# Two buffers for a convolution's copies, stores from another queue, and low parts of weights made half by VectorE and half by GpSimd

## The chip, the cores and the metric

The kernel runs on one core of one Trainium2 chip. The metric is device time in microseconds of one execution, the median of several runs. Engines are named as the profile names them: PE (TensorE), DVE (VectorE), ACT (ScalarE), POOL (GpSimd) and SP (SyncE, which here issues most transfers).

## The reference

The program computes two blocks on 512 tokens of 1024 channels: attention with a feed-forward layer, then a block of two branches (a gated depthwise convolution and a bidirectional state-space scan), followed by a mixture of 16 experts. The change lies in the second block's two branches:

```python
proj = einsum('btd,dk->btk', rms_norm(h, w_norm_mix), w_in)      # conf_a, conf_g, z, xbc, dt, gates
c = conf_a * sigmoid(conf_g)
c = depthwise_conv(c, w_conf_dw, b_conf_dw)                       # 31 taps, 1024 channels
branch_conf = silu(layer_norm(c)) @ w_conf_out
xbc = silu(depthwise_conv(xbc, w_ssm_conv, b_ssm_conv))           # 7 taps, 3072 channels
y = bidir_ssd(xs, dt, ..., Bs, Cs, ssm_d)                         # chunks of 128 tokens, 4 groups
branch_ssm = rms_norm(y * silu(z), w_ssm_norm) @ w_ssm_out
h = h + (gates[:D] * branch_conf + gates[D:] * branch_ssm) @ w_out
```

All inputs are float32.

## The kernel before, in words

Tokens lie along the free axis, in two halves of 264 (`HS`, 528 tokens with the meta tokens). Every projection is done by `lin2h`: a 128x1024 chunk of weights is loaded by SP into `wraw` (three buffers), ACT rounds it into a high part `whi` (L109, two buffers), and POOL subtracts that from `wraw` to get the low part `wlo` (L110, two buffers). PE then runs 48 matmuls per chunk, three for each of eight row blocks and each half: high by low (L142), low by high (L143), high by high (L144). ACT can write `whi` only after PE has done with the chunk two before.

After the norm, the stage makes the state-space inputs and runs four groups `g` of the scan. In each group a list of 16 steps (`ssd_steps`: `pre` on ACT, DVE and POOL, `mm` on PE) is laid out by hand, and `fill` spreads the other work evenly between the steps: the next group's convolved inputs (`convs`, whose seven taps per tile are DVE multiply-adds, L749, handed out by `background`), tiles of the gated product (`conf_tile`), the depthwise convolution's tiles (`conf_conv`), `z_tile` and `gate_tile`. PE's instructions run in this written order. The order on the other engines is made by the scheduler of the tile framework, which takes data dependences and buffers into account.

`conf_tile(m)` writes its product to DRAM (`rcD`). `conf_conv(m)` copies it back into `cz` in four pieces shifted by one token each (L909), loads its weights `cw` (L913), and runs 64 matmuls for each half of the tokens (L922) in which four taps lie on the partitions; the result `co` is stored to `cfD` (L928). `fetch(0)` stands ahead of the first half, `fetch(1)` is called when the first half's matmuls have been issued. Both `cz` and `cw` have one buffer. `gate_tile` stores its gate to `gD` (L951). In a scan step `y_rows` loads two broadcast rows (L817), `y_pre` makes the decay factors from them (ACT L830, DVE L833, POOL L842), and `y_mm` multiplies (L853); between the states of two chunks POOL and DVE carry `pv` on (L810, L811), and POOL makes `xe` (L798) for the states' matmuls (`stp`, L806). The rows of step j are loaded at the `pre` of two steps before. `ssp` is the stage's pool of buffers; `rp` are the inputs of the taps, cleared at their ends by POOL (L737).

Of the kernel before, what the change touches and what calls it, by code (L numbers as in the profile page):

```python
# [9 lines left out]
F32 = mybir.dt.float32  # L10
# [3 lines left out]
AF = mybir.ActivationFunctionType  # L14
# [3 lines left out]
P = 128  # L18
D = 1024
S = 512  # L20
T = 528
TH = 264
# [8 lines left out]
HS = [(0, TH), (TH, T)]  # L31
# [15 lines left out]
HALVES = (382, 383)  # L47
OFF = None
NBS = 6
NB = 6  # L50
LAMBDA_INIT = 0.8 - 0.6 * math.exp(0.0)
PV = {}
# [16 lines left out]
def body(ctx, tc, a, out):  # L69
    nc = tc.nc  # L70
    pe, act, dve, pool, sp = nc.tensor, nc.scalar, nc.vector, nc.gpsimd, nc.sync
# [20 lines left out]
    upool = pools(ctx)("upool", side="right")  # L92
    hpool = pools(hs)("hpool", side="right")

    wlast = []

    def wload(src, e):
        raw = wp.tile([P, 1024], F32, name="wraw", tag="wraw", bufs=3)
# [3 lines left out]
    def wchunk(src, kc, n=WC, raw=None):  # L102

        raw = raw or wload(src, kc * n)
        hi = wp.tile([P, 1024], F32R, name="whi", tag="whi", bufs=2)
        lo = wp.tile([P, 1024], F32R, name="wlo", tag="wlo", bufs=2)
        e = kc * n
        with tc.high_priority(OFF):
            act.copy(hi[:, :e], raw[:, :e])  # L109
            pool.tensor_sub(lo[:, :e], raw[:, :e], hi[:, :e])  # L110
        r = lambda t: t[:, :e].rearrange("p (k n) -> p k n", k=kc)
        return r(hi), r(lo)

# [14 lines left out]
    def V(name, i=0, n=1):  # L128
        o, w = PV[name]
        return pv[:, o + i:o + i + n]  # L130
# [343 lines left out]
    for u in range(len(units) + 2):  # L474
        if u < len(units):
            h, qi = units[u]
# [8 lines left out]
        if u >= 2:  # L485
            h, qi = units[u - 2]
# [49 lines left out]
    for m in range(NFF):  # L536
        pss = []
        for wn in ("w_gate", "w_up"):
            w = wchunk(a[wn][m], KD)
            ps = lin2.tile([P, 512], F32, name="fps", tag="f")  # L540
# [41 lines left out]
    w = wchunk(wd(KD - 1, 0), 8)  # L582
    for h in range(2):
        down_part(0, w, h)
    w = [wchunk(wd(KD - 1, i), (8, 6)[i - 1]) for i in (1, 2)]
# [53 lines left out]
    ssp = pools(b2s)("ssp")  # L639
# [74 lines left out]
    for h in range(2):  # L714
        for k in range(KD):
            for pss, wv, n in ((first[0], dtv, 64), (first[1], wB, P)):
                ps, s0, s1 = pss[h]
# [12 lines left out]
    def conv_ssm(tiles, first=None):  # L730

        rps = []

        def unit(i):
            m, dst = tiles[i]
            rp = ssp.tile([P, T + 6], F32, name="rp", tag="rp", bufs=3)
            pool.memset(rp[:, :3], 0.0)  # L737
            pool.memset(rp[:, T + 3:], 0.0)
            for ps, s0, s1 in (first if i == 0 and first else lin2h(lambda i: W2[32 + m], U)):
                act.activation(rp[:, 3 + s0:3 + s1], ps[:, :TH], AF.Copy, scale=0.5)  # L740
            act.activation(dst, rp[:, :T], AF.Identity, bias=hv[:, m:m + 1], scale=V("sw", m * 7))
            rps.append(rp)
            if i:
                for k in range(1, 7):
                    for x in range(2):
                        soon.append(lambda k=k, x=x: tap(k, *tiles[x], rps[x]))

        def tap(k, m, dst, rp):
            dve.scalar_tensor_tensor(dst, rp[:, k:k + T], V("sw", m * 7 + k), dst, ALU.mult, ALU.add)  # L749
            if k == 6:  # L750
                th = ssp.tile([P, T], F32, name="th", tag="th", bufs=2)
                act.activation(th, dst, AF.Tanh)
                dve.scalar_tensor_tensor(dst, th, 1.0, dst, ALU.add, ALU.mult)

        return [lambda: unit(0), lambda: unit(1)]
# [8 lines left out]
    def ssd_steps(g):  # L764
# [48 lines left out]
        def y_rows(c, q):  # L813
            n = CH[c][1] - CH[c][0]
            for d in range(2):
                row = ssp.tile([P, 4, P], F32, name=f"row{d}", tag=f"row{d}", bufs=3)
                sp.dma_start(out=row[:, :, :n], in_=rowD[d, c, 8 * g + 4 * q:8 * g + 4 * q + 4, :n].partition_broadcast(P))  # L817
                keep["row", c, q, d] = row
# [43 lines left out]
        pre, mm = [], []  # L862
# [7 lines left out]
        for j, (c, q) in enumerate(Y):  # L870
            pre.append([lambda c=c, q=q: y_pre(c, q)])
            mm.append([lambda c=c, q=q: y_mm(c, q)])
            pre[j + 4].insert(0, lambda c=c, q=q: y_rows(c, q))
            if q == 0 and c != CO[-1]:
                mm[-1].append(lambda c=c: cross(CO[CO.index(c) + 1]))
        return pre, mm

    cfD = dram.tile([P, KD, T], F32, name="cfD")
    rcD = dram.tile([KD, P, T + 31], F32, name="rcD")

    def conf_tile(m):

        th = []

        def gate_half():
            th.append(ssp.tile([P, T], F32, name="ct", tag="ct", bufs=1))
            for ps, s0, s1 in lin2h(lambda i: W2[8 + m], U):
                act.activation(th[0][:, s0:s1], ps[:, :TH], AF.Tanh, scale=0.5)

        def value_half():  # L890
            rp = ssp.tile([P, T + 31], F32, name="rcp", tag="rcp")
            pool.memset(rp[:, :15], 0.0)
            pool.memset(rp[:, T + 15:], 0.0)
            for ps, s0, s1 in lin2h(lambda i: W2[m], U):
                dve.scalar_tensor_tensor(rp[:, 15 + s0:15 + s1], th[0][:, s0:s1], 1.0, ps[:, :TH], ALU.add, ALU.mult)
            sp.dma_start(out=rcD[m], in_=rp)

        return [gate_half, value_half]

    def conf_conv(m):  # L900


        o = []

        def fetch(h):
            s0, s1 = HS[h]
            z = ssp.tile([P, 4, TH + 28], F32, name="cz", tag="cz")
            for j in range(4):
                sp.dma_start(out=z[32 * j:32 * j + 32],  # L909
                             in_=rcD[m][:, s0 + j:s1 + j + 28].rearrange("(b c) t -> c b t", c=32))  # L910
            if h == 0:
                w = ssp.tile([P, 8, 4, 32], F32, name="cw", tag="cw")
                sp.dma_start(out=w, in_=a["conf_dw"][m].rearrange("p (i b c) -> p i b c", i=8, b=4))  # L913
                o.extend((ssp.tile([P, T], F32, name="co", tag="co"), w, None))
            o[2] = z

        def taps(h):
            s0, s1 = HS[h]
            ps = lin.tile([P, 512], F32, name="l3", tag="lin")
            for i in range(8):  # L920
                for b in range(4):
                    pe.matmul(ps[32 * b:32 * b + 32, :TH], o[1][:, i, b, :], o[2][:, b, 4 * i:4 * i + TH],  # L922
                              start=i == 0, stop=i == 7, skip_group_check=True)
            act.activation(o[0][:, s0:s1], ps[:, :TH], AF.Identity, bias=V("cb", m), scale=0.5)
            if h == 0:
                fetch(1)
            else:
                sp.dma_start(out=cfD[:, m, :], in_=o[0])  # L928

        return [lambda: fetch(0), lambda: taps(0), lambda: taps(1)]  # L930

    def z_tile(m):
        th = ssp.tile([P, T], F32, name="zt", tag="zt")
# [10 lines left out]
    gD = dram.tile([16, P, T], F32, name="gD")  # L944

    def gate_tile(m, pl):
        th = pl.tile([P, T], F32, name="gt", tag="gt", bufs=1 if pl is ssp else 2)
        for ps, s0, s1 in lin2h(lambda i: W2[56 + m], U):
            act.activation(th[:, s0:s1], ps[:, :TH], AF.Tanh, scale=0.5)
        act.activation(th, th, AF.Copy, bias=0.5, scale=0.5)  # L950
        sp.dma_start(out=gD[m], in_=th)  # L951

    BC = {}
    CO = (2, 1, 3, 0, 4)
# [1 line left out]
    def convs(g, first=None):  # L956
        BC[g] = [ssp.tile([P, T], F32, name=n, tag=n, bufs=2) for n in ("Bt", "Ct")]
        r = conv_ssm([(16 + g, BC[g][0]), (20 + g, BC[g][1])], first)
        for i in (0, 2):
            r += conv_ssm([(4 * g + j, ys[:, 4 * g + j, :]) for j in (i, i + 1)])  # L960
        return r
# [2 lines left out]
    CT = [(2,), (3, 4), (5, 6), (7,)]  # L964
    CC = [(0, 1), (2,), (3, 4), (5, 6)]
    cv = convs(0, first[1])
    for f in cv[:4]:
        f()
    background(len(soon))
# [9 lines left out]
    for g in range(4):  # L979
# [10 lines left out]
        pre, mm = ssd_steps(g)  # L990
# [4 lines left out]
        for i in range(n):  # L995
# [7 lines left out]
            for f in mm[i]:  # L1003
                f()
            background(NB)
        background(len(soon))
# [7 lines left out]
    b2q.close()  # L1014


    b2n = ExitStack()
    nps = pools(b2n)("nps3", 4, psum=True)
    lw = pools(b2x)("lw")
# [12 lines left out]
    for s0, s1 in HS:  # L1032
        ps = nps.tile([P, 512], F32, name="ysp", tag="n")
# [16 lines left out]
    def ssm_out(m):  # L1050
        gt = gate(8 + m)
        pool.tensor_mul(gt, gt, rsy)
        bs[m] = lw.tile([P, T + 30], F32, name="bs", tag="bs", bufs=NBS)[:, :T]
        for ps, s0, s1 in lin2h(lambda i: a["w_ssm_out"][m, i], Y, (8, 8)):
# [9 lines left out]
    for s0, s1 in HS:  # L1064
        ps = nps.tile([P, 512], F32, name="mup", tag="n")
# [14 lines left out]
    for k in range(KD):  # L1080
        t = cf[:, k, :]
        th = lw.tile([P, T], F32, name="lt", tag="tmp", bufs=3)
# [5 lines left out]
        (pool if k % 2 else dve).tensor_sub(cl[:, k, :], t, ch[:, k, :])  # L1088
    for m in range(4, NBS):
        ssm_out(m)  # L1090
# [3 lines left out]
    for m in range(KD):  # L1094
        if NBS <= m + NBS - 1 < KD:
            ssm_out(m + NBS - 1)
        gt = gate(m)
        t = lw.tile([P, T], F32, name="mt", tag="tmp", bufs=3)
# [157 lines left out]
    for c, (c0, c1) in enumerate(CH):  # L1256
        col = aft[:, c, 0:1]
        for i, (s0, s1, op) in enumerate(((0, c1, ALU.is_ge), (c1, T, ALU.is_gt), (c0, c1, ALU.is_equal))):
            if s0 < s1:
                w = C["triu"][:, :c1 - c0] if i == 2 else C["ones"][:, :1].to_broadcast([P, s1 - s0])  # L1260
# [184 lines left out]
    ps = rps.tile([P, 512], F32, name="warm", tag="r")  # L1445
# [205 lines left out]
```

## Time and profile before

| | |
|---|---|
| median of three runs | 2659.17 us (2659.13 to 2660.89) |
| the profiled execution's own time, span | 2661.74 us, 2660.0 us |
| mean granted clock of PE | 0.973 |
| busy over the span: PE, DVE, ACT, POOL | 92%, 49%, 41%, 32% |

The profile is of one execution. An engine's busy time leaves out what it waits for. The stage of the change takes about 715 to 1400 us of the span; the experts' stage behind it streams its weights from DRAM.

### The profile page before, as it was taken

How to read it: one execution, taken by the hardware profiler on the slowest of the kernel's cores; microseconds unless marked ns; L12 is line 12 of the kernel's file. 1: busy time of each engine (PE TensorE's matmuls, PEld its weight loads, DVE VectorE, ACT ScalarE, POOL GpSimd, SP SyncE). 2: the span in 40 equal slices, each digit the busy share in tenths (PEclk: the TensorE clock that was granted, in tenths of full speed). 3: DMA queues.
4: the chain of work that ended last, by engine and by line, in shares of the span. 5: the costliest groups of instructions: out<-in, count | busy, mean ns of one | idle time of the engine just before them, and what ended most of it. 6: DMA issues, size and time to landing. Idle time of an engine off the chain costs nothing.

```text
span 2660.0 us, 65660 instructions
## 1 busy us (share of the span) xinstructions
PE 2448.3 (92%) x28940; PEld 2038.4 (77%) x28940; DVE 1299.6 (49%) x1673; ACT 1096.6 (41%) x1997; POOL 855.8 (32%) x649
## 2 busy tenths in 40 slices
PE   7999999999999799999899997999998988888897
PEld 6885688888888589887789996777776766776674
DVE  3536755532569484953446445344443333333345
ACT  5553532222454646374553322333333333333334
POOL 3543244444447566776535530000000000000000
PEclk9999999999999899999999998999999999999999
DMA  4211222232332525254433377999999999999996
GB/s 133 67 52 33 64 88 95 95 101 95 112 114 78 145 87 153 71 159 111 135 108 126 120 302 287 402 398 403 405 406 407 404 403 402 397 403 397 400 394 246
DMA packets 134363, 585.13 MB, mean 220 GB/s; under 512 B 24782, under 2 KB 33486, under 8 KB 84926
## 3 DMA queue, kind: packets, MB, share of 16 engines
q1 hardware_dynamic: 122352, 555.07, 55.7%
q10 hardware_dynamic: 8253, 17.40, 2.0%
q0 software_dynamic: 3472, 8.46, 1.4%
q8 instruction: 228, 3.74, 0.6%
q14 instruction: 58, 0.47, 0.1%
HBM read 559.28 MB, written 21.59 MB: 218 GB/s over the span
## 4 chain that ended last, share of the span: by engine, by line
PE 54%; DMA 26%; DVE 8%; issue 6%; ACT 3%; POOL 2%; SPq 0%; ACTq 0%; DVEq 0%; POOLq 0%
DMA eraw<-in_e_up_dram 9%; DMA eraw<-in_e_down_dram 7%; DMA eraw<-in_e_gate_dram 7%; PE eg L1346 6%; PE l L142 6%; PE l L144 6%; PE l L143 6%; PE fps L143 3%; PE fps L144 3%; PE fps L142 3%; PE lps L142 3%; PE lps L144 3%; PE lps L143 3%; PE l L922 2%; PE yp L853 2%
## 5 line engine op out<-in xcount | busy, mean ns | idle before, releaser
L110 POOL TENSOR_TENSOR wlo<-wraw,whi 128x1024 fp32r<-128x1024 f32 (+2 forms) x212 | 497.0, 2344 | 514.0 <-ACT whi L109 472.4
L1346 PEld LDWEIGHTS eg<-x,eraw 128*64 128x64 f32 x16384 | 509.7, 138 | 137.0 <-issue 106.1
L1346 PE MATMUL eg<-x,eraw 128*64 128x66 f32 x16384 | 537.9, 224 | 78.9 <-issue 33.8
L109 ACT CAST whi<-wraw 128x1024 fp32r<-128x1024 f32 (+2 forms) x212 | 213.3, 1006 | 481.4 <-issue 238.6
L1308 DVE TENSOR_TENSOR elo<-eraw,ehi 128x1024 fp32r<-128x1024 f32 x256 | 304.6, 1222 | 128.7 <-ACT ehi L1307 125.9
L142 PE MATMUL l<-uh,wlo 128*128 128x264 f32 x1152 | 340.9, 296 | 20.7 <-POOL wlo L110 14.5
L144 PE MATMUL l<-uh,whi 128*128 128x264 f32 x1152 | 332.6, 289 | 0.0
L143 PE MATMUL l<-ul,whi 128*128 128x264 f32 x1152 | 331.8, 288 | 0.0
L1307 ACT CAST ehi<-eraw 128x1024 fp32r<-128x1024 f32 x256 | 260.2, 1045 | 36.6 <-PE pd L144 27.6
L1317 POOL DMA_INDIRECT xg<-hnD,idx x16 | 15.8, 984 | 772.1 <-PE xtp L1334 638.0
L1472 DVE TENSOR_TENSOR ht<-eg,hx 128x132 f32<-128x132 f32 x128 | 37.8, 295 | 428.5 <-PE eg L1346 428.5
L142 PEld LDWEIGHTS l<-uh,wlo 128*128 128x128 f32 x1152 | 222.6, 193 | 29.7 <-POOL wlo L110 25.0
L143 PEld LDWEIGHTS l<-ul,whi 128*128 128x128 f32 x1152 | 222.5, 193 | 1.9 <-issue 1.4
L144 PEld LDWEIGHTS l<-uh,whi 128*128 128x128 f32 x1152 | 222.0, 193 | 0.0
L142 PE MATMUL pd<-ehi,hl 128*66 128x512 f32 x512 | 210.1, 410 | 8.8 <-ACT ehi L1307 3.8
L143 PE MATMUL pd<-elo,hh 128*66 128x512 f32 x512 | 203.3, 397 | 3.0 <-DVE hl L1474 1.3
L144 PE MATMUL pd<-ehi,hh 128*66 128x512 f32 x512 | 203.2, 397 | 0.0
L1473 ACT CAST hh<-ht 128x132 fp32r<-128x132 f32 x128 | 38.7, 302 | 329.4 <-DVE ht L1472 329.4
L1470 ACT ACTIVATE hx<-eg 128x132 f32<-128x132 f32 x128 | 35.9, 280 | 281.1 <-PE eg L1346 281.1
L142 PE MATMUL fps<-hh,wlo 128*128 128x512 f32 x352 | 138.7, 394 | 0.9 <-POOL wlo L110 0.9
L143 PE MATMUL fps<-hl,whi 128*128 128x512 f32 x352 | 139.3, 396 | 0.1
L144 PE MATMUL fps<-hh,whi 128*128 128x512 f32 x352 | 138.4, 393 | 0.0
(421 smaller groups left out, 4653.7 us busy)
## 6 DMA issues: line engine op xcount, KB each, us to landing
eraw<-in_e_up_dram SPq DMA_DIRECT2D x128, 1024.0 KB
eraw<-in_e_gate_dram SPq DMA_DIRECT2D x128, 1024.0 KB
eraw<-in_e_down_dram SPq DMA_DIRECT2D x126, 1024.0 KB
wraw<-in_w_in_dram SPq DMA_DIRECT2D x88, 512.0 KB
row<-rowD SPq DMA_DIRECT2D x64, 256.0 KB
wraw<-in_w_gate_dram SPq DMA_DIRECT2D x22, 512.0 KB
wraw<-in_w_up_dram SPq DMA_DIRECT2D x22, 512.0 KB
cz<-rcD SPq DMA_DIRECT2D x64, 146.0 KB
```

What stands on the lines that cost most here:

```text
L109: act.copy(hi[:, :e], raw[:, :e])
L110: pool.tensor_sub(lo[:, :e], raw[:, :e], hi[:, :e])
L142: pe.matmul(ps, sl, mh, start=first, stop=False)
L143: pe.matmul(ps, sh, ml, start=False, stop=False)
L144: pe.matmul(ps, sh, mh, start=False, stop=last)
L853: pe.matmul(yp[64 * (h % 2):64 * (h % 2) + 64, h // 2, :n], st[:, h * 64:h * 64 + 64], mv[:, h, :n], start=(o == 0 and h < 2), stop=(o == ...
L922: pe.matmul(ps[32 * b:32 * b + 32, :TH], o[1][:, i, b, :], o[2][:, b, 4 * i:4 * i + TH], start=i == 0, stop=i == 7, skip_group_check=True)
L1307: act.copy(hi, w[:, j, :])
L1308: dve.tensor_sub(lo, w[:, j, :], hi)
L1346: pe.matmul(ps[64 * h:64 * h + 64, j, :], w[:, k, P * j + 64 * h:P * j + 64 * h + 64], x[:, k, :], start=j == 0 and k == 0, stop=j == 1 an ...
L1472: dve.tensor_mul(ht, widen(x), hx)
L1473: act.copy(hid[0][:, s, :], ht)
```

## The change

There are five edits. While a flag is set (from the first convolved inputs of the stage to the end of the scan), `wchunk` gives the low part's columns 0 to 511 to DVE and columns 512 to 1023 to POOL. `conf_conv` fetches both halves at once into two buffers of `cz`, and then `cw`. The buffers `rcp`, `co` and `th` share one name with two buffers. The stores of `co` and of the gates are issued by ACT instead of SP. And the rows of a scan step are loaded one step before instead of two.

```diff
--- before.py
+++ after.py
@@ -47,6 +47,7 @@
 HALVES = (382, 383)
 OFF = None
 NBS = 6
+LOV = 512
 NB = 6
 LAMBDA_INIT = 0.8 - 0.6 * math.exp(0.0)
 PV = {}
@@ -92,7 +93,7 @@
     upool = pools(ctx)("upool", side="right")
     hpool = pools(hs)("hpool", side="right")
 
-    wlast = []
+    wlast, lo_dve = [], [False]
 
     def wload(src, e):
         raw = wp.tile([P, 1024], F32, name="wraw", tag="wraw", bufs=3)
@@ -107,7 +108,10 @@
         e = kc * n
         with tc.high_priority(OFF):
             act.copy(hi[:, :e], raw[:, :e])
-            pool.tensor_sub(lo[:, :e], raw[:, :e], hi[:, :e])
+            d = LOV if e == 1024 and lo_dve[0] else 0
+            pool.tensor_sub(lo[:, d:e], raw[:, d:e], hi[:, d:e])
+            if d:
+                dve.tensor_sub(lo[:, :d], raw[:, :d], hi[:, :d])
         r = lambda t: t[:, :e].rearrange("p (k n) -> p k n", k=kc)
         return r(hi), r(lo)
 
@@ -748,7 +752,7 @@
         def tap(k, m, dst, rp):
             dve.scalar_tensor_tensor(dst, rp[:, k:k + T], V("sw", m * 7 + k), dst, ALU.mult, ALU.add)
             if k == 6:
-                th = ssp.tile([P, T], F32, name="th", tag="th", bufs=2)
+                th = ssp.tile([P, T + 31], F32, name="th", tag="th", bufs=2)[:, :T]
                 act.activation(th, dst, AF.Tanh)
                 dve.scalar_tensor_tensor(dst, th, 1.0, dst, ALU.add, ALU.mult)
 
@@ -870,7 +874,7 @@
         for j, (c, q) in enumerate(Y):
             pre.append([lambda c=c, q=q: y_pre(c, q)])
             mm.append([lambda c=c, q=q: y_mm(c, q)])
-            pre[j + 4].insert(0, lambda c=c, q=q: y_rows(c, q))
+            pre[j + 5].insert(0, lambda c=c, q=q: y_rows(c, q))
             if q == 0 and c != CO[-1]:
                 mm[-1].append(lambda c=c: cross(CO[CO.index(c) + 1]))
         return pre, mm
@@ -888,7 +892,7 @@
                 act.activation(th[0][:, s0:s1], ps[:, :TH], AF.Tanh, scale=0.5)
 
         def value_half():
-            rp = ssp.tile([P, T + 31], F32, name="rcp", tag="rcp")
+            rp = ssp.tile([P, T + 31], F32, name="rcp", tag="th", bufs=2)
             pool.memset(rp[:, :15], 0.0)
             pool.memset(rp[:, T + 15:], 0.0)
             for ps, s0, s1 in lin2h(lambda i: W2[m], U):
@@ -902,32 +906,31 @@
 
         o = []
 
-        def fetch(h):
-            s0, s1 = HS[h]
-            z = ssp.tile([P, 4, TH + 28], F32, name="cz", tag="cz")
-            for j in range(4):
-                sp.dma_start(out=z[32 * j:32 * j + 32],
-                             in_=rcD[m][:, s0 + j:s1 + j + 28].rearrange("(b c) t -> c b t", c=32))
-            if h == 0:
-                w = ssp.tile([P, 8, 4, 32], F32, name="cw", tag="cw")
-                sp.dma_start(out=w, in_=a["conf_dw"][m].rearrange("p (i b c) -> p i b c", i=8, b=4))
-                o.extend((ssp.tile([P, T], F32, name="co", tag="co"), w, None))
-            o[2] = z
+        def fetch():
+            for s0, s1 in HS:
+                z = ssp.tile([P, 4, TH + 28], F32, name="cz", tag="cz", bufs=2)
+                for j in range(4):
+                    sp.dma_start(out=z[32 * j:32 * j + 32],
+                                 in_=rcD[m][:, s0 + j:s1 + j + 28].rearrange("(b c) t -> c b t", c=32))
+                o.append(z)
+            w = ssp.tile([P, 8, 4, 32], F32, name="cw", tag="cw")
+            sp.dma_start(out=w, in_=a["conf_dw"][m].rearrange("p (i b c) -> p i b c", i=8, b=4))
+            o.append(w)
 
         def taps(h):
             s0, s1 = HS[h]
+            if h == 0:
+                o.append(ssp.tile([P, T + 31], F32, name="co", tag="th", bufs=2)[:, :T])
             ps = lin.tile([P, 512], F32, name="l3", tag="lin")
             for i in range(8):
                 for b in range(4):
-                    pe.matmul(ps[32 * b:32 * b + 32, :TH], o[1][:, i, b, :], o[2][:, b, 4 * i:4 * i + TH],
+                    pe.matmul(ps[32 * b:32 * b + 32, :TH], o[2][:, i, b, :], o[h][:, b, 4 * i:4 * i + TH],
                               start=i == 0, stop=i == 7, skip_group_check=True)
-            act.activation(o[0][:, s0:s1], ps[:, :TH], AF.Identity, bias=V("cb", m), scale=0.5)
-            if h == 0:
-                fetch(1)
-            else:
-                sp.dma_start(out=cfD[:, m, :], in_=o[0])
-
-        return [lambda: fetch(0), lambda: taps(0), lambda: taps(1)]
+            act.activation(o[3][:, s0:s1], ps[:, :TH], AF.Identity, bias=V("cb", m), scale=0.5)
+            if h:
+                act.dma_start(out=cfD[:, m, :], in_=o[3])
+
+        return [fetch, lambda: taps(0), lambda: taps(1)]
 
     def z_tile(m):
         th = ssp.tile([P, T], F32, name="zt", tag="zt")
@@ -948,7 +951,7 @@
         for ps, s0, s1 in lin2h(lambda i: W2[56 + m], U):
             act.activation(th[:, s0:s1], ps[:, :TH], AF.Tanh, scale=0.5)
         act.activation(th, th, AF.Copy, bias=0.5, scale=0.5)
-        sp.dma_start(out=gD[m], in_=th)
+        act.dma_start(out=gD[m], in_=th)
 
     BC = {}
     CO = (2, 1, 3, 0, 4)
@@ -964,6 +967,7 @@
     CT = [(2,), (3, 4), (5, 6), (7,)]
     CC = [(0, 1), (2,), (3, 4), (5, 6)]
     cv = convs(0, first[1])
+    lo_dve[0] = True
     for f in cv[:4]:
         f()
     background(len(soon))
@@ -1014,6 +1018,7 @@
     b2q.close()
 
 
+    lo_dve[0] = False
     b2n = ExitStack()
     nps = pools(b2n)("nps3", 4, psum=True)
     lw = pools(b2x)("lw")
```

How this moves instructions is shown at three places. On SP, around the weights `cw` of convolution 1, first before (`cz_7116` is its first half, `cz_7193` its second, `co_6078` the result of convolution 0):

```order
L909 DMA cz_7116<-rcD_5198 32x4x292
L817 DMA row1_7019<-rowD_5085 128x512
L928 DMA cfD_5197<-co_6078 128x528
L909 DMA cz_7116<-rcD_5198 32x4x292 x3
L913 DMA cw_7121<-in_conf_dw_dram 128x1024
L817 DMA row1_7485<-rowD_5085 128x512
L817 DMA row1_7631<-rowD_5085 128x512
L817 DMA row1_7718<-rowD_5085 128x512
L909 DMA cz_7193<-rcD_5198 32x4x292 x4
```

and now (`cz_7140` is its second half, `cz_7473` the first half of convolution 2):

```order
L821 DMA row0_7111<-rowD_5085 128x512
L821 DMA row1_7034<-rowD_5085 128x512
L100 DMA wraw_7663<-in_w_in_2_dram 128x1024
L821 DMA row0_7652<-rowD_5085 128x512
L913 DMA cz_7140<-rcD_5198 32x4x292
L821 DMA row1_7113<-rowD_5085 128x512
L913 DMA cz_7140<-rcD_5198 32x4x292 x3
L917 DMA cw_7145<-in_conf_dw_dram 128x1024
L821 DMA row1_7654<-rowD_5085 128x512
L821 DMA row1_7742<-rowD_5085 128x512
L821 DMA row1_7839<-rowD_5085 128x512
L913 DMA cz_7473<-rcD_5198 32x4x292 x4
```

The store of `co` has left the queue, and ahead of `cw` now stand the copies of the second half; the four of the first half (`cz_7135`) stand ten rows earlier.

On DVE, among the taps ahead of the group loop, first before:

```order
L749 SCALAR_TENSOR_TENSOR ys<-rp,pv,ys 128x528 x6
L753 SCALAR_TENSOR_TENSOR ys<-th,ys 128x528
L749 SCALAR_TENSOR_TENSOR ys<-rp,pv,ys 128x528 x5
L753 SCALAR_TENSOR_TENSOR ys<-th,ys 128x528
L749 SCALAR_TENSOR_TENSOR ys<-rp,pv,ys 128x528 x7
L753 SCALAR_TENSOR_TENSOR ys<-th,ys 128x528
```

and now:

```order
L753 SCALAR_TENSOR_TENSOR ys<-rp,pv,ys 128x528 x4
L114 TENSOR_TENSOR wlo<-wraw,whi 128x512
L753 SCALAR_TENSOR_TENSOR ys<-rp,pv,ys 128x528 x3
L757 SCALAR_TENSOR_TENSOR ys<-th,ys 128x528
L753 SCALAR_TENSOR_TENSOR ys<-rp,pv,ys 128x528 x4
L114 TENSOR_TENSOR wlo<-wraw,whi 128x512
L757 SCALAR_TENSOR_TENSOR ys<-th,ys 128x528
L753 SCALAR_TENSOR_TENSOR ys<-rp,pv,ys 128x528 x6
L114 TENSOR_TENSOR wlo<-wraw,whi 128x512
L753 SCALAR_TENSOR_TENSOR ys<-rp,pv,ys 128x528
L757 SCALAR_TENSOR_TENSOR ys<-th,ys 128x528
```

DVE's halves of `wlo` stand between taps, about one to every five of them.

On POOL, in group 1, where `pv` is carried on and the next chunks' low parts are made, first before:

```order
L810 TENSOR_TENSOR pv_7267<-pv_7267,cd 128x512
L810 TENSOR_TENSOR pv_7268<-pv_7268,cd 128x512
L737 MEMSET rp 128x3
L738 MEMSET rp 128x3
L110 TENSOR_TENSOR wlo<-wraw,whi 128x1024
L798 TENSOR_TENSOR xe<-xTt,dd 128x512
L110 TENSOR_TENSOR wlo<-wraw,whi 128x1024
L798 TENSOR_TENSOR xe<-xTt,dd 128x512
```

and now:

```order
L814 TENSOR_TENSOR pv_7286<-pv_7286,cd 128x512
L846 TENSOR_TENSOR row_7740<-row_7740,Ct 128x512
L814 TENSOR_TENSOR pv_7287<-pv_7287,cd 128x512
L741 MEMSET rp 128x3
L742 MEMSET rp 128x3
L112 TENSOR_TENSOR wlo<-wraw,whi 128x512
L802 TENSOR_TENSOR xe<-xTt,dd 128x512
L112 TENSOR_TENSOR wlo<-wraw,whi 128x512
```

The multiply of a row stands between the two `pv` there, which before stood earlier, and the low parts are half as wide. PE's instructions are the same in the same order.

## Rows read from the trace of the kernel before

**Rows 1.** windows, the stage: PE, PEld, DVE, ACT, POOL busy (count), clock, DMA, GB/s

```profile
715.00:1400.00 685.00, 628.95 (x5908) 561.25 (x5907) 413.23 (x486) 366.49 (x847) 421.14 (x346) 0.95 0.39 117
```

**Rows 2.** PE's waits in 715:1400: in total us, times, longest us

```profile
PE l L922 <- DMA cz<-rcD: 16.1, 3, 6.7
PE l L142 <- POOL wlo L110: 14.5, 6, 4.8
PE l L922 <- DMA cw<-in_conf_dw_dram: 10.1, 1, 10.1
...
PE stp L806 <- POOL xe L798: 3.6, 2, 2.7
```

**Rows 3.** the chain in 690:1460: start us, us, what

```profile
884.86 7.38 DMA cw<-in_conf_dw_dram
892.33 5.96 PE l L922 x64
...
903.50 5.45 PE l L922 x64
...
1193.73 3.74 PE l L922 x64
...
1203.09 5.89 PE l L922 x64
...
1308.52 6.08 PE l L922 x64
```

**Rows 4.** windows, the slow L922 group at 1203.09

```profile
1203.09:1208.98 5.89, 5.89 (x66) 2.95 (x68) 0.00 (x0) 0.00 (x0) 0.00 (x0) 0.63 0.00 0
```

**Rows 5.** timeline of SP in 860:906 and 1190:1213: start us, us, what

```profile
881.35 0.37 SPq L928 DMA_DIRECT2D cfD<-co  x1
881.76 2.18 SPq L909 DMA_DIRECT2D cz<-rcD  x3
...
1197.49 11.85 SPq L909 DMA_DIRECT2D cz<-rcD  x5
```

**Rows 6.** costliest groups by shape, POOL and DVE: busy us, mean ns, idle before

```profile
L110 POOL TENSOR_TENSOR wlo<-wraw,whi 128x1024 fp32r<-128x1024 f32 x188 | 461.5, 2455 | 430.3 <-ACT whi L109 396.5 <-issue 27.6 <-DMA cf<-cfD 3.3
L110 POOL TENSOR_TENSOR wlo<-wraw,whi 128x512 fp32r<-128x512 f32 x16 | 20.8, 1302 | 60.7 <-ACT whi L109 53.0 <-ACT lm L362 4.3 <-issue 3.4
L842 POOL TENSOR_TENSOR row<-row,Ct 128x512 f32<-128x512 f32 x56 | 79.3, 1432 | 40.1 <-ACT row L841 39.9
...
L749 DVE SCALAR_TENSOR_TENSOR ys<-rp,pv,ys 128x528 f32<-128x528 f32 x96 | 112.0, 1168 | 4.9 <-ACT ys L741 2.3
L134 DVE TENSOR_TENSOR mix<-o,mix 128x512 fp32r<-128x512 f32 x4 | 2.7, 680 | 2.1 <-ACT mix L133 2.1
```

**Rows 7.** timeline of DVE and POOL in 738:750

```profile
741.09 0.71 DVE L753 SCALAR_TENSOR_TENSOR ys<-th,ys 128x528 f32<-128x528 f32 x1
...
746.47 2.49 DVE L753 SCALAR_TENSOR_TENSOR ys<-th,ys 128x528 f32<-128x528 f32 x1 [0.71 <-ACT th L752]
...
746.05 2.35 POOL L110 TENSOR_TENSOR wlo<-wraw,whi 128x1024 fp32r<-128x1024 f32 x1
```

**Rows 8.** windows, tiles of `lin2h` (48 matmuls each) by tile l

```profile
748.45:762.61 14.16, 14.15 (x96) 13.94 (x96) 0.00 (x0) 1.15 (x3) 0.82 0.27 89
816.68:822.77 6.09, 6.08 (x48) 5.87 (x48) 0.00 (x0) 0.00 (x0) 1.00 0.26 86
963.85:972.04 8.19, 8.19 (x48) 7.97 (x48) 0.00 (x0) 0.39 (x1) 0.72 0.39 130
1106.42:1114.96 8.54, 8.54 (x48) 8.33 (x48) 0.00 (x0) 1.14 (x3) 0.68 0.18 64
```

**Rows 9.** windows, sums over four stretches: all engines, then tile wlo alone

```profile
sum 254.00, PE 232.25 PEld 209.41 DVE 237.59 ACT 105.74 POOL 171.00; mean PE 58.06 PEld 52.35 DVE 59.40 ACT 26.43 POOL 42.75
...
sum 254.00, PE 138.95 PEld 90.78 POOL 76.57; mean PE 34.74 PEld 22.70 POOL 19.14
```

## The prediction

> **What bounds the kernel now.** I read the page's busy times first: TensorE (PE) is far the busiest engine of the whole span (table above). All edits lie in the state-space stage, about 715 to 1400 us, so the next view is that stretch alone: PE is busy 628.95 of 685 us, idle 56, the other engines are busy 366 to 421 us [rows 1]. So the stage is as long as PE's matmuls plus PE's holes, and since PE's order of instructions is the same before and after, the change can only fill or make holes. Third comes the list of PE's waits in that stage. The reader is to see that three sorts of work release nearly all of them: the copies `cz` for the convolution (three waits, 16.1 us), the low parts `wlo` made by POOL (six, 14.5 us), the convolution's weights `cw` (one, 10.1 us), and `xe`, POOL again (two, 3.6 us) [rows 2]. Together 44.3 us.
>
> A hole costs more than its own length. The chain shows the 64-matmul group of L922 as 3.74 us where PE ran on without a hole, and 5.45, 5.89 and 6.08 us behind a wait for `cz`, 5.96 us behind the one for `cw` [rows 3]. The stretch of the 5.89 us group has a granted clock of 0.63 [rows 4], one in which PE had not stood (816.68) 1.00 [rows 8]: behind a hole PE ran part of the group at the lower of its two levels, 1.2 instead of 2.4 GHz. So each hole removed ahead of L922 gives back its length and about 2 us more.
>
> Then I followed the holes to their causes. In SyncE's (SP's) queue the second half's first copy is issued 3.8 us after PE began the first half's matmuls, since the one `cz` buffer is free only then; PE stands until the data has landed; the fifth issue of the 11.85 us is the next convolution's first copy, which in turn waits for the second half's matmuls [rows 3, 5]. Late `wlo` has another cause. POOL's subtraction of a 128x1024 tile takes 2455 ns, a half tile 1302 [rows 6], and one tile in every 6.08 us of PE's matmuls [rows 8] would be no load; but VectorE (DVE) and POOL don't run side by side there. A DVE multiply-add at 741.09 us took 0.71 us; the same line at 746.47, begun 0.42 us after POOL's `wlo`, took 2.49 and ended 0.56 us after POOL's 2.35 were over (748.96 against 748.40) [rows 7].
>
> **The change part by part.**
>
> *Copies in two buffers.* The three `cz` waits go, 16.1 us, and the slow groups behind them become 3.74 us: 5.45 + 5.89 + 6.08 - 3 x 3.74 = 6.2. Sum 22.3 us. Both halves are now asked for together, and in SP's order the second half's four copies stand right before `cw`. The bound on the good side is the whole 22.3. On the poor side the second half of convolution 1 still waits as now (3.74 hole and 1.71 slowness) and a few us return as waits of a first half behind more copies: 14. I take 22, since the first halves never waited for `cz` so far, and a second half landing one group later than the first has 3.7 us of matmuls more.
>
> *The wait for `cw`.* `cw` has one buffer, so that of convolution 1 still can't be asked for until the second taps of convolution 0 are done. Before, it was issued at 884.86, behind the store of `co` (881.35) and three copies (from 881.76, 2.18 us) [rows 5]. Now the store is out of SP's queue, and the four copies ahead of `cw` are the second half's; the first half's stand ten rows earlier. What is saved is at least the 0.41 us from the store to the copies, at most the 3.5 us from the store to `cw`; what is added is the load of the second half's copies, issued just ahead of it. I take 1 us of gain, bounds 3.5 and -2 (a quarter of its 7.38 us, for 0.58 MB of copies beside it). About 9 us of this hole stay.
>
> *Half of `wlo` by DVE.* It concerns 65 tiles. The row of the 128x512 half says 1302 ns for POOL; for DVE I take the row `mix<-o,mix`, the same operation, shape and types: 680 ns [rows 6]. If DVE and POOL exclude each other, as [rows 7] show, a tile takes 1.30 + 0.68 = 1.98 us of the two instead of 2.455: 0.47 less. The low parts that PE waits for lie in four stretches (717:764, 788:860, 919:989, 1065:1130) with 30 tiles, 76.57 us of POOL; DVE is busy there 237.59 of 254 us, PE idle 21.75 [rows 9]. 30 x 0.47 = 14 us of engine time are freed, about 4 are taken by the three `row` multiplies that, by POOL's order, the later row loads bring into the beginnings of two groups (three of 1432 ns [rows 6]), so 10 net. A hole closes only by what the tile that it waits for gains, though: six waits for `wlo` and two for `xe` by 0.47 each are 4, and 1 us for slow matmuls behind them. I take 5. On the good side all of these holes and their slowness vanish. A tile's 48 matmuls take 6.08 us where PE has not stood; behind three of the holes one tile took 8.54, one 8.19 and a pair 14.15 [rows 8], together 6.6 too many. With 14.5 and 3.6 that is 24.7. On the poor side the tile is complete later than now (third rival); -6 here, that is 0.2 us on each of 30 tiles.
>
> The rule that speaks against this part: the Trainium skill, page "SBUF — State Buffer", section "SBUF: two separate sides", says that DVE operations with two SBUF inputs and GpSimd operations reading SBUF lock one shared port pair for a whole instruction, so the loser stands still rather than slowed. The trace agrees (2.49 us beside 0.71). By that rule the two halves add; by the engines' rows taken side by side the tile would take 1.30 alone, which is the second rival.
>
> *Stores from ScalarE's (ACT's) queue.* 24 issues leave SP, 18 of them in the loop over the groups (8 of `cfD`, 10 of `gD`); one takes 0.37 us on SP [rows 5], so some 7 us go from SP to ACT there. ACT is busy 366.49 of 685 us [rows 1], so the issues lie in its idle time. On SP the store no longer holds up what stands behind it. By the order, 11 of them wait in ACT's queue for an earlier transfer too, and behind them stand the casts. I take 2 us of loss, bounds 0 (all transfers long done) and 11 (one us each, since SP's own issues wait for transfers too).
>
> *Shared buffers, later rows.* `rcp`, `th` and `co` in two buffers of one name can make a tanh wait for a store; the tanh of the taps waits for DVE already. The rows are asked for one step (685 us over 64 steps, 10.7) ahead instead of two, still longer than the 7.38 us that `cw`, twice a row's size, took in a crowded stretch [rows 3]. I put both at nothing: what hides them is the work of that step, and if it doesn't suffice where SP is blocked, as behind five copies in 11.85 us [rows 5], about a us at each of the eight convolutions is lost, 8 us at worst.
>
> Sum against the profiled execution's 2661.74 us: -22 - 1 - 5 + 2 = -26, that is 2635.7. The median of the runs is 2.57 lower than that execution: **2633 us**. What is gained here passes to the end, as PE remains the bound of what follows and the later weight loads stand behind this stage in SP's queue.
>
> **The rivals.**
>
> *The wait moves to the first half (chance 0.18).* Eight copies (32x4x292 floats each) and `cw` (128x1024 floats) are 1.7 MB, where `cw` alone, 0.52 MB, took 7.38 us [rows 3]. For it: SP's order, in which `cw`, without which no half can start, stands behind all eight. Against it: the first half's four were there before too, and where the buffers are free all eight are only earlier. If the first halves then wait some 4 to 5 us at three places, 14 of the 22 go: 2661.74 - 8 - 1 - 5 + 2 - 2.57 = 2647.
>
> *Halves side by side (0.12).* If DVE's instruction doesn't block POOL's of this kind, a tile takes 1.30 us in place of 2.455, 1.15 less, more than the holes ask for; then all 24.7 go instead of 5: -22 - 1 - 24.7 + 2 = -45.7, and 2661.74 - 45.7 - 2.57 = 2613.5. Against it stand [rows 7].
>
> *DVE's half is late: slower (0.10).* DVE does its work in order and is 94% busy in the four stretches [rows 9]. A half stands in that queue between multiply-adds of 1168 ns [rows 6], behind one it comes that much later; and if it is reached early, DVE stands until ACT has made `whi`, which itself waits for PE to leave the buffer, and the multiply-adds behind it, with POOL's clearing of `rp`, get late. At one multiply-add for each of the 30 tiles, 35 us are lost, where 5 were to be gained: -22 - 1 + 2 + 35 = +14, 2673. It makes the kernel slower from (21 + 5.3) / 30 = 0.9 us per tile on.
>
> *About the same (0.05):* a loss by late halves that eats up what is left in the first rival.
>
> **How the numbers follow.** My forecast has 0.55, with 2622 to 2645 as its own range. About 0.2%, 5.3 us, is what a measurement of this kernel tells from no change. The forecast, the side-by-side case and most of the first rival are faster: 0.83. Same 0.09 (the last case, a bit of the first and of the third), slower 0.08. The range leaves out the third rival and half of the second: 2612 to 2655.
>
> **What would show it.** The waits for `cz` gone from PE's list and every L922 group but that behind `cw` at 3.7 to 3.8 us; one wait for `cw` of 8 to 10 us remains; the DVE half at 0.68 us alone and near 2 beside POOL; POOL's halves at about 1.3; waits for `wlo` shorter but not gone, some named after DVE's line. I am wrong if first halves wait for `cz` or `cw` at more than one place, if PE's waits for `wlo` exceed 18 us, if DVE's waits for ACT's `whi` show up before its half, or if ACT's casts stand behind a store.

## The result, and the profile after

The changed kernel takes 2629.72 us (median of four runs, 2627.98 to 2632.37) against 2660.03 us of the kernel before beside it: ratio 0.9882, 95% interval 0.987 to 0.9895. It is 30 us faster; 2633 was forecast, and 2612 to 2655 as the range. The profiled execution took 2627.98 us.

The list of PE's waits in the stage, which now ends some 35 us earlier (columns as in [rows 2]):

```profile
PE l L146 <- DVE wlo L114: 9.1, 4, 4.5
PE l L927 <- DMA row<-rowD: 8.4, 1, 8.4
PE l L146 <- ACT gt L952: 6.3, 1, 6.3
PE stp L810 <- POOL xe L802: 3.4, 2, 2.2
...
PE yp L857 <- POOL row L846: 1.2, 1, 1.2
PE yp L857 <- DVE M L837: 1.1, 2, 0.6
```

The waits for `cz` are gone. One long hole ahead of the convolution is left, under another name (`row`, an inference of the profile; the fourth experiment shows that it is `cw`). Of `wlo` there remain four waits by DVE's half, and none that POOL's half ends in this window. Behind the hole for the convolution the group is slow as before, elsewhere it isn't; first two rows of PE's timeline, then three of the chain:

```profile
870.00 3.77 PE L927 MATMUL l<-cz,cw 128*32 128x264 f32 x64
...
884.39 6.07 PE L927 MATMUL l<-cz,cw 128*32 128x264 f32 x64 [8.38 <-DMA row<-rowD]
```

```profile
1175.60 7.26 PE l L927 x128
...
1270.46 3.70 PE l L927 x64
1275.62 3.74 PE l L927 x64
```

The group of 128 at 1175.60 is the two halves one behind the other, where before 5.6 us of hole and a group of 5.89 us stood between them [rows 3]. The two engines and the halves of one tile, where nothing else is in the way (timeline of DVE, then POOL):

```profile
973.99 0.69 DVE L114 TENSOR_TENSOR wlo<-wraw,whi 128x512 fp32r<-128x512 f32 x1 [1.65 <-ACT whi L110]
```

```profile
974.04 1.78 POOL L112 TENSOR_TENSOR wlo<-wraw,whi 128x512 fp32r<-128x512 f32 x1 [2.26 <-ACT whi L110]
```

Both begin within 0.05 us of each other when `whi` is ready; DVE takes its 0.69 us, POOL 1.78 instead of the 1.28 to 1.30 that other halves of it take alone. The tile is complete 1.86 us after `whi` (ready at 973.96), neither 1.30 nor 2.4. In all twelve tiles of the stage whose halves both begin within 0.13 us of `whi` it is 1.86 to 1.91 us. The groups by shape are longer in the mean, which I put down to other work of the two engines beside them (mean ns of one after the comma):

```profile
L114 DVE TENSOR_TENSOR wlo<-wraw,whi 128x512 fp32r<-128x512 f32 x65 | 61.1, 940 | 71.9 <-ACT whi L110 65.2 <-issue 6.6
...
L112 POOL TENSOR_TENSOR wlo<-wraw,whi 128x512 fp32r<-128x512 f32 x65 | 105.0, 1615 | 68.8 <-ACT whi L110 51.7 <-issue 17.0
```

Since PE has the same 28940 matmuls in the same order in every kernel here that doesn't change them, its traces can be laid on each other: the start of the nth matmul, less that of the nth in the trace of before. A step down between two rows is time won in between.

```
us in before  what stands there        after  copies alone  low parts alone
 706.07       stage begins             -1.2      -2.7           -2.6
 761.72       behind the first taps    -5.5      -2.7           -6.9
 850.54       group 0                  -8.1      -1.1           -8.6
 892.33       L922, convolution 1      -7.9      -1.5           -9.3
 912.04       behind its second half  -13.3      -7.5           -9.3
 974.11       group 1                 -18.0      -8.8          -15.1
1196.82       end of L922 at 1193     -18.1      -9.1          -15.7
1213.91       behind the next L922    -26.2     -17.1          -15.9
1300.98       L922 at 1296            -26.2     -17.1          -15.9
1320.99       behind the next L922    -35.3     -26.2          -18.5
1382.50       end of the stage        -35.2     -26.1          -18.8
2648.47       near the end            -33.4     -25.9          -18.1
```

What is won sits at the three second halves (5.4, 8.0, 9.1 us) and in the stretches of the taps. At the end 1.8 us less is left; in the experts' stage the difference goes up and down by 1 to 2 us. None of these kernels has an edit ahead of the stage, so I take the 1 to 3 us there as the spread between executions. From the stage's beginning to its end the change wins 34.0 us, the copies alone 23.4 and the low parts alone 16.2: together they are 5.6 us short of the sum.

### The profile page after: what moved, and what is told of

The parts are those of the page before. It is cut to its first block, busy times and chain, and to the rows that moved or that the text cites. A ratio compares the mean times of both kernels' runs of the same rounds, so it can differ in the third digit from the quotient of the medians.

```text
span 2626.1 us, 65762 instructions
## 1 busy us (share of the span) xinstructions
PE 2427.9 (92%) x28940; PEld 2025.9 (77%) x28940; DVE 1300.0 (50%) x1738; ACT 1102.4 (42%) x1998; POOL 801.1 (31%) x649
## 4 chain that ended last, share of the span: by engine, by line
PE 54%; DMA 29%; DVE 8%; issue 4%; ACT 3%; POOL 1%; ACTq 0%; SPq 0%; DVEq 0%; POOLq 0%
DMA eraw<-in_e_up_dram 10%; DMA eraw<-in_e_down_dram 8%; DMA eraw<-in_e_gate_dram 8%; PE eg L1351 7%; PE l L146 6%; PE l L148 5%; PE l L147 5%; PE fps L147 3%; PE fps L148 3%; PE fps L146 3%; PE lps L146 3%; PE lps L148 3%; PE lps L147 3%; DVE ys L753 2%; PE yp L857 2%
## 5 line engine op out<-in xcount | busy, mean ns | idle before, releaser
L112 POOL TENSOR_TENSOR wlo<-wraw,whi 128x1024 fp32r<-128x1024 f32 (+2 forms) x212 | 435.6, 2055 | 519.6 <-ACT whi L110 490.2
L1322 POOL DMA_INDIRECT xg<-hnD,idx x16 | 15.8, 986 | 774.3 <-PE xtp L1339 640.0
L146 PEld LDWEIGHTS l<-uh,wlo 128*128 128x128 f32 x1152 | 220.3, 191 | 23.4 <-DVE wlo L114 11.9
```

Of the source, the lines that this page charges most:

```text
L112: pool.tensor_sub(lo[:, d:e], raw[:, d:e], hi[:, d:e])
L146: pe.matmul(ps, sl, mh, start=first, stop=False)
```

## The experiments

All times are medians of four or five runs; ratios are to the kernel before on the same chip in the same rounds.

**1 and 2. Each half of the change alone.** The copies alone: the changed `fetch`, `taps` and shared buffers put into the kernel before, with the store left on SP.

> The kernel before with the copies edit alone: both halves fetched at once into two buffers of cz, then cw; rcp, th and co share two buffers. Low parts all on POOL, stores on SP, rows two steps ahead. My theory: the three waits for cz (16.1 us) and the slow groups behind them (6.2) go, whatever else is edited: 2660 - 22 = 2638, no L922 group but the one behind cw over 3.8 us. Rival: the copies gain only because the stores have left SP's queue; then one or more cz waits stay and the time is 2645 to 2655.

2642.27 us, ratio 0.9929 (0.9916 to 0.9943). The waits in its stage:

```profile
PE l L142 <- POOL wlo L110: 15.0, 6, 4.8
PE l L923 <- DMA row<-rowD: 9.7, 1, 9.7
...
PE stp L806 <- POOL xe L798: 2.9, 2, 2.1
```

No `cz` is left and POOL's holes are untouched. The three steps in the table (6.0, 8.0 and 9.1 us) are 23.1 us. The rival falls: the copies need no store to leave SP. The median gains only 17.7, between my 22 and the rival's 5 to 15, though: two of its five runs took 2635.3 and 2635.4 us and three 2642.3 to 2642.9; the profiled one is of the shorter. What sets these two apart isn't known.

> The kernel before with half of each low part on DVE and nothing else. My theory: DVE and POOL take turns, a tile is ready 0.5 us sooner, and only the holes behind wlo and xe shorten: -5 to -10 us, 2650 to 2655; the three cz waits and the cw wait stay. Rival (halves side by side): all 24.7 us of holes and slowness behind POOL go, 2635. Rival (DVE's half late): 2660 or more.

```diff
+            d = LOV if e == 1024 and lo_dve[0] else 0
-            pool.tensor_sub(lo[:, :e], raw[:, :e], hi[:, :e])
+            pool.tensor_sub(lo[:, d:e], raw[:, d:e], hi[:, d:e])
+            if d:
+                dve.tensor_sub(lo[:, :d], raw[:, :d], hi[:, :d])
```

2644.14 us, ratio 0.9948 (0.9934 to 0.9961): 15.8 us, where I expected 5 to 10 and the side-by-side rival some 25.

```profile
PE l L926 <- DMA cz<-rcD: 14.5, 3, 5.6
PE l L926 <- DMA row<-rowD: 10.4, 1, 10.4
PE l L146 <- DVE wlo L114: 9.2, 4, 4.5
```

The convolution's holes stay, though the three for `cz` are 1.6 us shorter than before. By the medians the two parts give 17.7 and 15.8 alone, together 33.5 against 30.3 in one, which is within the spread; by the table they overlap by 5.6 us. Part of that is the last second half, where the low parts alone win 2.6 us of a hole that the copies remove whole.

**3, 9, 10. How many columns go to DVE.** `LOV` of 1024 (POOL's subtraction left out where it has no column), 0 and 768, all else as in the changed kernel.

> The changed kernel with the low parts on POOL alone again (0 of 1024 columns on DVE). It gives the first point of a line: 0 columns here, 512 in the changed kernel (2629.7), 768 next, 1024 on DVE alone (2614.5). My theory: DVE and POOL take turns, so a tile is ready after about 2.4, 1.9, 1.6 and 1.2 us and the time falls with each step: here 2638 to 2644, near the copies alone (2642.3). Rival: the halves gain only where POOL's own queue is long, and the later rows and the stores have eased that already: 2632 to 2637.

> The changed kernel with 768 of 1024 columns on DVE and 256 on POOL. Turns theory: between 512 and 1024 columns, 2619 to 2625. Rival: what made 1024 columns better is that a tile no longer needs both engines' queues (PE waits for the later of two); then 768 columns, which need both, are not better than 512: 2628 to 2632.

> The changed kernel with whole low parts on DVE, none on POOL, in the same stage. If the two engines take turns and their common time is what counts, a tile takes about 1.2 us instead of 1.9 and the kernel gains a little more: 2622 to 2628. If DVE's order is what counts (work behind taps, DVE busy 94% of the crowded stretches), 0.5 us more of DVE for each of 65 tiles makes it 2632 to 2645.

| columns on DVE | us | ratio (95%) |
|---|---|---|
| 0 | 2640.54 | 0.9922 (0.9909 to 0.9935) |
| 512 (the change) | 2629.72 | 0.9882 (0.987 to 0.9895) |
| 768 | 2619.89 | 0.9847 (0.9834 to 0.986) |
| 1024 | 2614.49 | 0.983 (0.9817 to 0.9844) |

The time falls with every step, as it would if the two take turns and DVE is the quicker worker (the intervals of 768 and 1024 touch); a tile that needs both engines' queues (768) is not worse than 512. For 1024 I had expected 2622 to 2628; it is 7.5 us faster than the lower end, an expectation that fell short as the low parts' term did (below). PE's waits for low parts in the stage with 0 columns, then with 1024:

```profile
PE l L146 <- POOL wlo L112: 15.1, 6, 4.8
```

```profile
PE stp L811 <- POOL xe L803: 2.9, 3, 1.1
...
PE l L147 <- DVE wlo L115: 1.8, 2, 1.5
```

With 1024 columns the whole subtraction takes DVE 1334 ns in the mean, but a tap takes 890 where it was 1168 [rows 6]. DVE is busy less in the four crowded stretches, 223.54 us where it was 237.59 [rows 9], when they are taken between the same matmuls (713.0:753.6, 777.7:845.5, 897.9:961.0, 1036.8:1096.0):

```profile
L115 DVE TENSOR_TENSOR wlo<-wraw,whi 128x1024 fp32r<-128x1024 f32 x65 | 86.7, 1334 | 78.9 <-ACT whi L110 78.8
L754 DVE SCALAR_TENSOR_TENSOR ys<-rp,pv,ys 128x528 f32<-128x528 f32 x96 | 84.8, 890 | 2.0
```

```profile
sum 230.70, PE 221.99 PEld 200.51 DVE 223.54 ACT 121.10 POOL 106.18; mean PE 55.50 PEld 50.13 DVE 55.88 ACT 30.27 POOL 26.54
```

**4. Which transfer the last hole waits for.**

> The changed kernel with the second load of cw left out: convolution 1 uses the weights of convolution 0, so its result is not the reference's. The changed kernel's profile names a row load as releaser of the 8.4 us hole ahead of that convolution. My theory: it is cw; without its load the hole goes, with the slow group behind it (6.07 instead of 3.77): 2629.7 - 10.7 = 2619. Rival: what PE waits for is the row loads or the second half's copies in the same queue; the hole stays within 2 us, 2627 to 2630.

```diff
+            if m == 1:
+                o.append(cw0[0])
+                return
             w = ssp.tile([P, 8, 4, 32], F32, name="cw", tag="cw")
...
+            cw0[:] = [w]
             o.append(w)
```

2622.57 us, ratio 0.9866 (0.9851 to 0.9881), 7 us less than the changed kernel where 10.7 were expected; the intervals touch, so the trace has to tell. PE's timeline at the place:

```profile
873.57 3.77 PE L933 MATMUL l<-cz,cw 128*32 128x264 f32 x64
...
880.24 3.77 PE L933 MATMUL l<-cz,cw 128*32 128x264 f32 x64 [1.44 <-DMA cz<-rcD]
```

The hole and its slow group are gone, the row loads are all still there: it was `cw`. Laid on the changed kernel's trace, 9.3 us are won between 706 and 912 us, of which the second half's 1.44 us of waiting is already taken off; by 974 us 6.6 are left, since the holes of group 1, which DVE and POOL set, take the rest back.

**5 and 6. The stores and the rows, undone.** The two `act.dma_start` are `sp.dma_start` again; `pre[j + 5]` is `pre[j + 4]`.

> The changed kernel with the stores of co and of the gates back on SP. My theory: this part is worth nothing or little on PE's path: 2628 to 2633, the holes of PE in the same places within 1 us. Rival: the stores hold up the copies in SP's queue, as cfD did by 0.41 us and more; waits for cz or cw come back and the time is 2634 to 2640.

2628.23 us, ratio 0.9872 (0.9855 to 0.9888): no difference that can be told.

> The changed kernel with the rows of a scan step loaded two steps before again. PE's times in the changed kernel fall back by 1.9 us between 851 and 876 of the kernel before, where PE waits for POOL's row multiply (1.2) and DVE's M (1.1), and its gain around 941 to 974 is 3 us where the low parts alone gave 5.9. My theory: the later rows cost 2 to 5 us; undone, 2625 to 2628. Rival: those are POOL's low parts in another order by chance, and the rows earlier only fill SP's queue ahead of copies: 2630 to 2634.

2629.32 us, ratio 0.9876 (0.986 to 0.9893): none either. My expectation here was wrong; the wait of `yp` for POOL's row stays at 1.2 us with the rows earlier:

```profile
PE l L146 <- DVE wlo L114: 9.0, 4, 4.5
...
PE yp L857 <- POOL row L846: 1.2, 1, 1.2
PE yp L857 <- DVE M L837: 1.0, 2, 0.6
```

**7, 8, 11. Against the hole of `cw`.** In `cw_mid` the load of `cw` is moved from behind the loop over the halves into it:

```diff
                 o.append(z)
+                if h == 0:
+                    w = ssp.tile([P, 8, 4, 32], F32, name="cw", tag="cw")
+                    sp.dma_start(out=w, in_=a["conf_dw"][m].rearrange("p (i b c) -> p i b c", i=8, b=4))
```

> The changed kernel with cw asked for between the first half's copies and the second half's instead of behind both. In the changed kernel cw is issued at 877.87 behind three copies that begin at 875.10, and PE's hole ends at 884.39. My theory: cw is issued and lands about 3 us sooner, the hole is 5 to 6 us: 2626 to 2628, and no second half waits. Rival: the transfer is what takes the time, with the copies beside it as before: hole still 7.5 or more, 2629 to 2630; or the second half waits in its place.

2626.24 us, ratio 0.9862 (0.9846 to 0.9879). SP's queue:

```profile
874.45 0.33 SPq L918 DMA_DIRECT2D cw<-in_conf_dw_dram  x1
875.34 0.32 SPq L821 DMA_DIRECT2D row<-rowD  x1
875.72 12.97 SPq L913 DMA_DIRECT2D cz<-rcD  x8
```

`cw` is issued at 874.45, 3.4 us earlier than in the changed kernel, and the hole is 5.16 us instead of 8.38; it ends at 881.78. The row loads that stand behind `cw` in the changed kernel come behind all eight copies here, after the hole, so they were not what PE waited for. On the matmuls laid on each other it is 3.6 us ahead of the changed kernel by 912 us, 0.8 of which it had before the stage, and 0.9 by 974: the holes of group 1, which DVE and POOL set, take it back. The interval overlaps the changed kernel's, so the time alone doesn't tell them apart.

> Whole low parts on DVE (2614.5 us so far) and two buffers for cw, with the rows of a scan step in two buffers instead of three to make room. The hole of 8.9 us ahead of convolution 1 and its slow group (5.38 instead of 3.77) go: 2604, or 2608 if the rows in two buffers make PE wait 4 us more at yp. If the rows' buffers are what the steps need, 2615 or more.

`bufs=2` for `cw`, `bufs=2` instead of 3 for the rows, low parts as in the third: 2626.44 us, ratio 0.9862 (0.9843 to 0.9882). The hole ahead of convolution 1 (8.90 us in the third) is gone, and yet the kernel is 12 us slower than the third. More than that is lost where a step's rows come late; two of PE's waits, then one of ACT's that isn't among the long ones of the third:

```profile
PE yp L858 <- DVE M L838: 7.7, 5, 3.0
...
PE l L928 <- DVE zt L940: 5.0, 2, 3.4
```

```profile
ACT M L835 <- DMA row<-rowD: 39.3, 23, 5.3
```

So this version says that the third buffer of the rows is needed, and doesn't price a second buffer of `cw` by itself. Its four runs lie 10 us apart (2622 twice, 2631 twice), so the 12 us are rough.

> Whole low parts on DVE and cw asked for between the two halves' copies: the two single edits that gained. If they add, 2614.5 - 3.5 = 2611; if the earlier cw is given back at the next hole as its trace showed in part, 2613 to 2615.

2613.42 us, ratio 0.9818 (0.9805 to 0.983), against 2614.49 with whole low parts on DVE alone: the best of all, by no more than the spread. The earlier `cw` is given back at the next hole: on the matmuls laid on each other this kernel is 2.2 us ahead of the third by 912 us and level by 974.

## Why the prediction was right, point by point

**Copies: right, in mechanism and, by the traces, in size.** 22 us were taken; the three places give 22.5 in the changed kernel and 23.1 with the copies alone, whose median gains only 17.7. All groups but that behind `cw` run at 3.70 to 3.77 us, so hole and slowness went together, as [rows 3, 4] let one expect. The first rival, a wait that moves to a first half, did not come: no first half waits for more than before.

**`cw`: right.** About 9 us were to stay; the hole is 8.4 us with a slow group of 6.07. That is 1.7 us less hole than before [rows 2], where 1 was taken: in this trace the copies ahead of it cost no more than the store's leaving saved. With the stores back on SP (fifth experiment) the hole is 9.7 us. The load is issued 2.8 us behind the first of three copies (875.10 and 877.87):

```profile
875.10 2.23 SPq L913 DMA_DIRECT2D cz<-rcD  x3
877.87 0.35 SPq L917 DMA_DIRECT2D cw<-in_conf_dw_dram  x1
```

**Low parts: right that the two engines take turns; the term was half of what it should have been.** The forecast took 5 us. Between 0 and 512 columns the medians differ by 10.8, and the two traces by 10.0 in the stage (24.0 and 34.0 us won). The turns held: 1.86 us a tile where 1.98 was worked out. The Trainium skill's page "SBUF — State Buffer", section "SBUF: two separate sides", says that the shared ports are an exclusive lock for a whole instruction, not a split of bandwidth. The trace agrees: beside DVE's 0.69 us POOL's half of the same tile is 0.48 to 0.50 us longer than alone, and the tile's 1.86 us are near the sum of the two (1.97 to 1.99), not the larger (1.30).

What failed is the next step, "a hole closes only by what the tile that it waits for gains", 0.47 us for each. The hole before that ended at 748.45 shows it. It was 3.85 us long and is gone. The first line is from the trace before, the others are from the one after:

```profile
745.91 0.10 POOL L737 MEMSET rp<- 128x3 f32 x1 [5.33 <-DVE ys L749]
```

```profile
742.21 0.68 DVE L114 TENSOR_TENSOR wlo<-wraw,whi 128x512 fp32r<-128x512 f32 x1
742.43 0.10 POOL L741 MEMSET rp<- 128x3 f32 x1 [5.21 <-DVE ys L753]
742.58 1.47 POOL L112 TENSOR_TENSOR wlo<-wraw,whi 128x512 fp32r<-128x512 f32 x1
743.26 0.28 PE L146 MATMUL l<-uh,wlo 128*128 128x264 f32 x1
```

Two things beside the tile's own time closed it. First, a backlog: POOL's clearing of `rp`, which stands ahead of the low part in its queue and waits for DVE's taps, comes 3.5 us earlier (742.43 against 745.91), of which 1.2 are from before the stage; what the tiles before it freed arrives here. Second, PE doesn't wait for a whole tile. Columns 0 to 511 are the chunk's first four row blocks, so PE begins with DVE's half alone (done at 742.89) and needs POOL's, done at 744.05, only twelve matmuls later. At the places of three holes before (748.45, 816.68 and 963.85) PE now begins 0.79, 1.06 and 1.08 us ahead of the end of POOL's half, and the holes behind `wlo` are gone: by that some 3 of the 10 us, an estimate from these three differences, hang on which half goes to DVE. No run has the halves exchanged.

The estimate one step earlier in the same paragraph, 10 us net over the 30 tiles, is met in number, but it counts neither PE's early beginning nor the new holes below. For 768 and 1024 columns it is 20.7 and 26 us less than for none, the latter near the 24.7 that all these holes and their slowness cost.

**DVE's half late: the third rival, there at all four waits that are left.** POOL's half of the tile was done 4.5, 0.6, 2.1 and 4.2 us before PE's wait ended; DVE's half ended each. The six waits before lose 9.2 of their 14.5 us, but waits of 1.73 and 2.10 us stand where none stood before. The second is there with the copies alone too (2.49 us, behind POOL). The first is new with the halves; it ends at 750.95, because DVE does taps while POOL's half is long done:

```profile
744.54 5.76 DVE L753 SCALAR_TENSOR_TENSOR ys<-rp,pv,ys 128x528 f32<-128x528 f32 x6
744.99 1.46 POOL L112 TENSOR_TENSOR wlo<-wraw,whi 128x512 fp32r<-128x512 f32 x1 [0.94 <-ACT whi L110]
750.21 0.68 DVE L114 TENSOR_TENSOR wlo<-wraw,whi 128x512 fp32r<-128x512 f32 x1
750.95 0.39 PE L146 MATMUL l<-uh,wlo 128*128 128x264 f32 x1 [1.73 <-DVE wlo L114]
```

With whole low parts on DVE there is no wait at this place, and the stretch from 740 to 762 us wins 6.4 us instead of 4.3. The longest hole behind `wlo` before, 4.81 us, which ended at 1106.42, is still 4.52 us long and ends at 1088.20. Its `whi` was ready at 1078.72, POOL's half at 1083.97; DVE's queue held its half until 1087.47:

```profile
1079.82 1.54 DVE L757 SCALAR_TENSOR_TENSOR ys<-th,ys 128x528 f32<-128x528 f32 x1
1081.29 5.66 DVE L753 SCALAR_TENSOR_TENSOR ys<-rp,pv,ys 128x528 f32<-128x528 f32 x5
1086.87 0.68 DVE L815 TENSOR_TENSOR pv<-stp,pv 128x512 f32<-128x512 f32 x1
1087.47 0.68 DVE L114 TENSOR_TENSOR wlo<-wraw,whi 128x512 fp32r<-128x512 f32 x1
```

Here it costs nothing new, since POOL's own queue had held the tile as long before; with all columns on DVE the hole is 1.5 us. DVE also waits 65.2 us before its halves for ACT's `whi`, which the forecast named as a sign of being wrong; it was no loss, because all but 0.2 us of it lies outside the four crowded stretches.

**Stores and rows: right to put them near nothing.** The 2 us of loss by ACT's issues can't be seen.

Added up by the traces, the parts are 22.5 for the copies, 1.6 for `cw` and 10 for the low parts, 34 us, as the profiled pair shows (33.8); the medians differ by 30.3. The forecast of -26 is so the sum of a term that was right and one that was 5 us too small, with 2 us of loss that did not come. That 2633 lies only 3 us from the 2629.72 measured is in part luck: the profiled pair is the slowest execution before and the fastest after, and against its 33.8 us the forecast is 8 us short.

## What to carry to other kernels

Where two engines take turns at a port, count their times as one queue; of the four shares tried here, the best for the slower engine was none. A hole at the end of a crowded stretch closes by what the whole stretch saves, not by what the last item saves, up to the hole's length, and work that is split in order of use lets the reader begin with the first part. A half on a busy engine also comes late: look at which half ends last at each wait. And a second buffer pays where the load waits for the last reader and PE for the load; it brings the length of the hole and the slow matmuls behind it.

## What was not expected

The releaser that the profile names for a wait on several transfers was wrong by name (`row` for `cw`), and only leaving the transfer out, or moving it, told so. More work on DVE lowered DVE's busy time (237.59 to 223.54 us between the same matmuls), as the busy time of an engine that stands at the port counts the standing. And the third buffer of the rows, which looked idle once the rows were asked for a step later, was worth about 12 us or more: with two buffers ACT waits 39.3 us for rows, whatever step the code asks in.
